# Turning queries and keys with block transfers and one VectorE transpose in a two-layer decoder trunk

## The chip, the cores and the metric

The kernel runs on one core of a Trainium2 chip. The time of a run is device microseconds (us). The engines of the core work side by side, each through its own list of instructions in order: TensorE (PE in the profile; PEld is its weight load), VectorE (DVE), ScalarE (ACT), GpSimd (POOL) and SyncE (SP), which issues the transfers.

## What is computed

A residual stream x of 256 rows and 2048 columns passes through two layers. Each layer norms x, projects it onto queries, keys (in the second layer forget gates), values and a gate for each of 32 heads, mixes within each head, and projects the result back. Cut to the lines that matter here:

```python
def even_layer(x, norm_g, w_in, q_gain, k_gain, w_out):
    proj = jnp.einsum('bsd,de->bse', rms_norm(x, norm_g), w_in)
    qa, ka, va, qb, kb, vb, gate = split_cols(proj, ...)
    oa = stick_breaking_attention(to_heads(qa), to_heads(ka), to_heads(va))   # 16 heads
    ob = dilated_attention(to_heads(qb), to_heads(kb), to_heads(vb), q_gain, k_gain)  # 16 heads
    mix = jnp.concatenate([oa, ob], axis=-1) * jax.nn.silu(gate)
    return x + jnp.einsum('bse,ed->bsd', mix, w_out)

def odd_layer(x, norm_g, w_in, lb, o_gain, w_out):
    proj = jnp.einsum('bsd,de->bse', rms_norm(x, norm_g), w_in)
    q, f_pre, inp, gate = split_cols(proj, ...)
    o = hgrn2(to_heads(q), to_heads(f_pre), to_heads(inp), lb)                # 32 heads
    mix = rms_norm(o, o_gain) * jax.nn.silu(gate)
    return x + jnp.einsum('bse,ed->bsd', mix, w_out)
```

Both attentions multiply queries with keys over the 128 head columns, and hgrn2 forms its scores from queries and keys with running products of the forget gates along the rows. Each of these wants the head's columns on the 128 partitions, while the projection leaves its rows there.

## The kernel before

For each head a product of 16 steps (`product`, L247) adds 128x512 matmuls into two PSUM tiles `acc`, one for each half of the 256 rows. The 512 columns are the head's query, key or forget gate, value and gate, 128 each. A step is six matmuls. The weights come in pairs of steps: one transfer (`raw`, L200), one ScalarE cast to the high part (`whi`, L211) and one VectorE subtraction to the low part (`wlo`, L212). Four buffers each of `raw`, `whi` and `wlo` are in use, so the cast for pair p+4 waits until TensorE is done with pair p. Here the pairs of a head are called pair 0 to pair 7.

The work that follows a head's product runs beside the product of the next head. It is a Python generator; `Side.tick` resumes it between steps, and `yield n` puts it off by n steps. A scheduler then fixes the order of each engine's list. Each head goes through these places:

- `evacuate` (L272) copies `acc`, scaled, to an SBUF tile `pj`, two ScalarE instructions of 512 columns.
- `flip_pair` (L140) transposes query and key with four TensorE transposes against `ident` into one PSUM tile (`flip`, L137); ScalarE then copies them to SBUF.
- A stick-breaking head (L305) multiplies them at L313 and L314, a dilated head (L338) at L358 and L359.
- An hgrn head (L390) takes sigmoids of the forget gate, then runs a chain of about 20 VectorE instructions from L401 to L454 that makes `sp`, `qk` and `qv`, and TensorE forms two sets of scores from them at L461 (the second one from `qv`).
- `weighted_values` (L295) and `emit_mix` (L291) end the head; the latter transposes the result `sg`.

Of the kernel before, what the change touches and what calls it, by code (L numbers as in the profile page):

```python
# [10 lines left out]
F32 = mybir.dt.float32  # L11
# [23 lines left out]
def hybrid_trunk(  # L35
# [16 lines left out]
    nc = tc.nc  # L52
    const = ctx.enter_context(tc.tile_pool(name="const", bufs=1))
# [15 lines left out]
    lbr = const.tile([P, 2, NH], F32, name="lbr")  # L69
    ones = const.tile([P, SEQ], F32, name="ones")  # L70
    nc.vector.memset(ones, 1.0)
    ident = const.tile([P, P], F32, name="ident")
# [67 lines left out]
    def flip_pair(pj):  # L140

        ps = flip([pj[:, t, c * P : (c + 1) * P] for c in range(2) for t in range(NT)])
        return ps.rearrange("p (c t) -> p c t", c=2)

# [133 lines left out]
    def gate_exp(pj):  # L278

        g = pj[:, :, 384:512]  # L280
# [13 lines left out]

    def weighted_values(at0, at1, at11, pj, c):  # L295


        o = psb.tile([P, NT, P], F32, name="att")
        v = pj[:, :, c * P : (c + 1) * P]
        nc.tensor.matmul(o[:, 0, :], at0, v[:, 0, :], start=True, stop=True)  # L300
        nc.tensor.matmul(o[:, 1, :], at1, v[:, 0, :], start=True, stop=False)  # L301
        nc.tensor.matmul(o[:, 1, :], at11, v[:, 1, :], start=False, stop=True)  # L302
        return o

    def stick_breaking(h, pj):  # L305
        sg = gate_exp(pj)
        yield 4
        ps = flip_pair(pj)
        qk = work.tile([P, 2, SEQ], F32, name="qk", bufs=2)
        nc.scalar.copy(qk, ps)  # L310
        yield 3
        zp = psb.tile([P, 384], F32, name="att")
        nc.tensor.matmul(zp[:, 0:128], qk[:, 0, 0:P], qk[:, 1, 0:P], start=True, stop=True)  # L313
        nc.tensor.matmul(zp[:, 128:384], qk[:, 0, P:], qk[:, 1, :], start=True, stop=True)  # L314
        z = work.tile([P, 384], F32, name="wt", bufs=2)
        nc.vector.scalar_tensor_tensor(
            z, zp, 1.0 / math.sqrt(P), strict, op0=ALU.mult, op1=ALU.add
        )
        sp = work.tile([P, 384], F32, name="qv", bufs=2)
        nc.scalar.activation(sp, z, AF.Abs)  # L320
        nc.scalar.activation(sp, sp, AF.Exp, scale=-1.0)
        nc.scalar.activation(sp, sp, AF.Ln, bias=1.0)
        nc.vector.scalar_tensor_tensor(sp, z, 0.0, sp, op0=ALU.max, op1=ALU.add)

        for lo, hi in ((0, 128), (128, 384)):
            back = sp[:, lo:hi][:, ::-1]
            nc.vector.tensor_tensor_scan(back, ones[:, 0 : hi - lo], back, 0.0, ALU.mult, ALU.add)
# [5 lines left out]
        o = weighted_values(at[:, 0:128], at[:, 128:256], at[:, 256:384], pj, 2)  # L333
        nc.vector.tensor_mul(sg, o, sg)
        yield 2
        emit_mix(h, sg, 1.0)

    def dilated(h, pj):  # L338
        sg = gate_exp(pj)
        qv = pj[:, :, 0:256].rearrange("p t (c d) -> p t c d", c=2)  # L340
        sq = work.tile([P, NT, 2, P], F32, name="sp", bufs=2)
# [6 lines left out]
        for t in range(NT):  # L348
            sl = pj[:, t, P : 2 * P]
# [7 lines left out]
        z = psb.tile([P, 384], F32, name="att")  # L357
        nc.tensor.matmul(z[:, 0:128], qk[:, 0, 0:P], qk[:, 1, 0:P], start=True, stop=True)  # L358
        nc.tensor.matmul(z[:, 128:384], qk[:, 0, P:], qk[:, 1, :], start=True, stop=True)  # L359
        nm = small.tile([P, NT], F32, name="nm")  # L360
# [20 lines left out]
        yield 3  # L381
        o = weighted_values(at[:, 0:128], at[:, 128:256], at[:, 256:384], pj, 2)
        for t in range(NT):
# [5 lines left out]

    def hgrn(h, pj):  # L390
        g = pj[:, :, 384:512]
# [12 lines left out]
        nc.scalar.activation(kk, fp, AF.Sigmoid, scale=-1.0)  # L404
        q = work.tile([P, SEQ], F32, name="qt", bufs=2)
        nc.scalar.copy(q, ps[:, 0, :])
        nc.scalar.activation(kk, kk, AF.Copy, scale=oml[:, h : h + 1])

        def blocks(a, n):
            return a.rearrange("p (b n) -> p b n", n=n)  # L410

# [30 lines left out]
        qq, cross = qc[:, 0:SEQ], qc[:, SEQ:]  # L442
        nc.vector.tensor_mul(qq, q, f)

# [75 lines left out]
        yield 2  # L520
        o = weighted_values(at[:, 0, :], cross, at[:, 1, :], pj, 2)
        so = small.tile([P, NT], F32, name="so")
# [178 lines left out]
```

## Time and profile before

| what | value |
|---|---|
| median of 3 runs | 1967.46 us (1967.27 to 1967.49) |
| profiled execution | 1967.47 us |
| its span | 1965.7 us |
| PE busy | 1956.2 us (100%) |
| DVE busy | 1286.5 us (65%) |
| ACT busy | 1038.3 us (53%) |
| POOL busy | 55.9 us (3%) |
| DMA moved | 344.39 MB, mean 175 GB/s |

The span reaches from the first instruction to the last. The profiled execution took 1.77 us more than its span. The granted clock was 1.0 (of 2.4 GHz) throughout.

### The profile page before, as it was taken

How to read it: one execution, taken by the hardware profiler on the slowest of the kernel's cores; microseconds unless marked ns; L12 is line 12 of the kernel's file. 1: busy time of each engine (PE TensorE's matmuls, PEld its weight loads, DVE VectorE, ACT ScalarE, POOL GpSimd, SP SyncE). 2: the span in 40 equal slices, each digit the busy share in tenths (PEclk: the TensorE clock that was granted, in tenths of full speed). 3: DMA queues.
4: the chain of work that ended last, by engine and by line, in shares of the span. 5: the costliest groups of instructions: out<-in, count | busy, mean ns of one | idle time of the engine just before them, and what ended most of it. 6: DMA issues, size and time to landing. Idle time of an engine off the chain costs nothing.

```text
span 1965.7 us, 25693 instructions
## 1 busy us (share of the span) xinstructions
PE 1956.2 (100%) x9280; PEld 1611.5 (82%) x9280; DVE 1286.5 (65%) x2456; ACT 1038.3 (53%) x1653; POOL 55.9 (3%) x54
## 2 busy tenths in 40 slices
PE   8999999999999999999999999999999999999999
PEld 7888888888888888888888888888888888888887
DVE  6666666666666666555577777777777777776444
ACT  6555555555555555444455555555555555555432
POOL 0000000000000000000000000000000000000000
PEclk9999999999999999999999999999999999999999
DMA  9555555555555555555554544555555544455664
GB/s 324 166 178 175 173 174 177 173 172 175 177 173 173 175 176 172 181 183 192 187 177 161 162 160 161 172 161 165 166 163 162 165 162 160 158 169 164 200 204 139
DMA packets 97407, 344.39 MB, mean 175 GB/s; under 512 B 11136, under 2 KB 12288, under 8 KB 97280
## 3 DMA queue, kind: packets, MB, share of 16 engines
q1 hardware_dynamic: 97136, 342.73, 54.0%
q8 instruction: 73, 1.20, 0.2%
q14 instruction: 54, 0.44, 0.1%
q10 hardware_dynamic: 144, 0.02, 0.0%
HBM read 340.61 MB, written 2.10 MB: 174 GB/s over the span
## 4 chain that ended last, share of the span: by engine, by line
PE 100%; DMA 0%; ACT 0%; DVE 0%; DVEq 0%; issue 0%
PE acc L254 30%; PE acc L256 30%; PE acc L255 30%; PE att L137 3%; PE att L461 2%; PE att L490 1%; PE att L301 1%; PE att L302 1%; PE att L300 1%; PE att L518 0%; PE att L359 0%; PE att L314 0%; DMA gn<-in_gains 0%; PE att L313 0%; PE att L358 0%; ACT xh L128 0%
## 5 line engine op out<-in xcount | busy, mean ns | idle before, releaser
L212 DVE TENSOR_TENSOR wlo<-raw,whi 128x1024 fp32r<-128x1024 f32 (+1 forms) x642 | 782.2, 1219 | 545.2 <-ACT whi L211 543.8
L211 ACT CAST whi<-raw 128x1024 fp32r<-128x1024 f32 (+1 forms) x642 | 673.2, 1049 | 631.6 <-PE acc L256 547.2
L254 PE MATMUL acc<-whi,xh 128*128 128x512 f32 x2048 | 837.4, 409 | 5.8 <-ACT whi L211 5.8
L256 PE MATMUL acc<-whi,xl 128*128 128x512 f32 x2048 | 802.6, 392 | 0.0
L255 PE MATMUL acc<-wlo,xh 128*128 128x512 f32 x2048 | 800.1, 391 | 0.0
L256 PEld LDWEIGHTS acc<-whi,xl 128*128 128x128 f32 x2048 | 384.9, 188 | 84.9
L254 PEld LDWEIGHTS acc<-whi,xh 128*128 128x128 f32 x2048 | 385.7, 188 | 79.0 <-ACT whi L211 5.8
L255 PEld LDWEIGHTS acc<-wlo,xh 128*128 128x128 f32 x2048 | 386.3, 189 | 72.0 <-DVE wlo L212 0.6
L254 PE MATMUL acc<-whi,mixh 128*128 128x512 f32 x512 | 201.8, 394 | 0.0
L256 PE MATMUL acc<-whi,mixl 128*128 128x512 f32 x512 | 199.5, 390 | 0.0
L255 PE MATMUL acc<-wlo,mixh 128*128 128x512 f32 x512 | 199.3, 389 | 0.0
L256 PEld LDWEIGHTS acc<-whi,mixl 128*128 128x128 f32 x512 | 96.1, 188 | 20.3
L255 PEld LDWEIGHTS acc<-wlo,mixh 128*128 128x128 f32 x512 | 96.2, 188 | 19.4
L254 PEld LDWEIGHTS acc<-whi,mixh 128*128 128x128 f32 x512 | 96.2, 188 | 19.3
L275 ACT ACTIVATE pj<-acc,rstd 128x512 f32<-128x512 f32 x128 | 87.5, 685 | 30.6 <-PE acc L256 30.1
L285 DVE RECIPROCAL sg<-sg 128x256 f32<-128x256 f32 x32 | 56.0, 1749 | 0.5
L179 POOL TENSOR_TENSOR rr<-rv,mhalf 128x4 f32<-128x4 f32 x16 | 29.3, 1833 | 716.0 <-DVE rv L178 716.0
L179 POOL TENSOR_TENSOR ro<-rv,mhalf 128x2 f32<-128x2 f32 x32 | 25.0, 780 | 831.0 <-DVE pr L474 808.0
L504 ACT COPY ri<-qk 128x128 f32<-128x128 f32 x32 | 9.6, 299 | 58.4 <-DVE qk L413 58.4
L137 PE MATMUL att<-ident,pj 128*128 128x128 f32 x256 | 38.5, 272 | 0.0
L413 DVE TENSOR_TENSOR qk<-qk 128x128 f32<-128x128 f32 x128 | 37.0, 289 | 2.2
L429 DVE RECIPROCAL ri<-qk 128x160 f32<-128x160 f32 x32 | 36.7, 1148 | 0.0
(141 smaller groups left out, 1272.3 us busy)
## 6 DMA issues: line engine op xcount, KB each, us to landing
raw<-in_w_odd SPq DMA_DIRECT2D x256, 512.0 KB, 3.6
raw<-in_w_even SPq DMA_DIRECT2D x254, 512.0 KB, 3.5
raw<-in_w_out SPq DMA_DIRECT2D x128, 512.0 KB, 3.5
xres<-in_xt SPq DMA_DIRECT2D x8, 256.0 KB, 7.3
xres<-in_x SPq DMA_DIRECT2D x4, 512.0 KB, 7.3
out<-xres SPq DMA_DIRECT2D x6, 256.0 KB, 5.1
raw<-in_w_even SPq DMA_DIRECT2D x4, 256.0 KB, 4.8
out<-xres SPq DMA_DIRECT2D x4, 128.0 KB, 2.0
```

What stands on the lines that cost most here:

```text
L137: nc.tensor.transpose(ps[:, i * P : (i + 1) * P], b, ident)
L179: nc.gpsimd.tensor_tensor(dst, v[:, 0:n], mhalf[:, 0:n], op=ALU.pow)
L211: nc.scalar.copy(hi[:, s, :], half[:, s, :])
L212: nc.vector.tensor_sub(lo[:, s, :], half[:, s, :], hi[:, s, :].bitcast(F32))
L254: nc.tensor.matmul(acc[t], sh[:, k, s], hi, start=(k == 0), stop=False)
L255: nc.tensor.matmul(acc[t], sh[:, k, s], lo, start=False, stop=False)
L256: nc.tensor.matmul(acc[t], sl[:, k, s], hi, start=False, stop=(k == nk - 1))
L275: nc.scalar.activation(pj[:, t, :], acc[t], AF.Copy, scale=rstd[:, t : t + 1])
L285: nc.vector.reciprocal(sg, sg)
L413: nc.vector.tensor_tensor(o, a, b.broadcast_to(list(o.shape)), op=ALU.mult)
L429: nc.vector.reciprocal(ri, f8[:, :, 3:8])
L461: nc.tensor.matmul(ps[:, t, :], kt[:, t * P : (t + 1) * P], qt[t], start=True, stop=True)
```

## The change

Queries and keys leave PSUM into a tile of their own (`qkp`), values and gates into another (`pj`, half as wide). 16 SBUF-to-SBUF transfers for each head, issued from SP, each move one 32-row by 32-column block of four 128x128 squares to its transposed place in a tile `mvp` (one buffer). One VectorE transpose then turns each 32x32 block. The last head of the dilated group and the last hgrn head keep the TensorE transposes (`quick`). The yields around the place change: in a stick-breaking head 4 before the flips becomes 2 before the moves and 4 before the turn, in a dilated head 8 becomes 5 and 4, in an hgrn head 3 becomes 2 and 4. A vector of 256 ones becomes one element that is broadcast.

```diff
+    def move_blocks(src, name):
+        n = src.shape[2] // P
+        moved = work.tile([P, NT, n, 4, 32], F32, name=name, bufs=1)
+        to = moved.rearrange("p t c a j -> p (t c) a j")
+        v = src.rearrange("p t (c f) -> p (t c) f", f=P)
+        for a in range(4):
+            for b in range(4):
+                nc.sync.dma_start(
+                    to[32 * b : 32 * b + 32, :, a, :], v[32 * a : 32 * a + 32, :, 32 * b : 32 * b + 32]
+                )
+        return moved
+    def turn_blocks(dst, moved):
+        nc.vector.transpose(dst, moved.rearrange("p t c a j -> p (t c a j)"))
+    def turn_pair(qk, quick):
+        if quick:
+            ps = flip([qk[:, t, c * P : (c + 1) * P] for t in range(NT) for c in range(2)])
+            nc.scalar.copy(qk, ps.rearrange("p (t f) -> p t f", t=NT))
+        else:
+            moved = move_blocks(qk, "mvp")
+            yield 4
+            turn_blocks(qk.rearrange("p t f -> p (t f)"), moved)
...
     def evacuate(acc, rstd):
-        pj = work.tile([P, NT, 512], F32, name="pj", bufs=2)
-        for t in range(NT):
-            nc.scalar.activation(pj[:, t, :], acc[t], AF.Copy, scale=rstd[:, t : t + 1])
-        return pj
+        qk = work.tile([P, NT, 256], F32, name="qkp", bufs=2)
+        vg = work.tile([P, NT, 256], F32, name="pj", bufs=2)
+        for dst, c in ((qk, 0), (vg, 256)):
+            for t in range(NT):
+                nc.scalar.activation(
+                    dst[:, t, :], acc[t][:, c : c + 256], AF.Copy, scale=rstd[:, t : t + 1]
+                )
+        return qk, vg
...
-    def stick_breaking(h, pj):
-        sg = gate_exp(pj)
-        yield 4
-        ps = flip_pair(pj)
-        qk = work.tile([P, 2, SEQ], F32, name="qk", bufs=2)
-        nc.scalar.copy(qk, ps)
+    def stick_breaking(h, qk, vg):
+        sg = gate_exp(vg)
+        yield 2
+        yield from turn_pair(qk, False)
         yield 3
...
-        yield 8
-        ps = flip_pair(pj)
-        qk = work.tile([P, 2, SEQ], F32, name="qk", bufs=2)
-        nc.scalar.copy(qk[:, 0, :], ps[:, 0, :])
-        nc.scalar.activation(qk[:, 1, :], ps[:, 1, :], AF.Copy, scale=qkg)
+        yield 5
+        yield from turn_pair(qk, h == NH - 1)
+        k = qk[:, :, P:]
+        nc.scalar.activation(k, k, AF.Copy, scale=qkg)
         yield 3
...
-        yield 3
-        ps = flip_pair(pj)
-        fp = ps[:, 1, :]
+        yield 2
+        yield from turn_pair(qk, h == NH - 1)
+        q, fp = qk[:, :, 0:P], qk[:, :, P:]
         fk = work.tile([P, 2, SEQ], F32, name="qk", bufs=2)
         f, kk = fk[:, 0, :], fk[:, 1, :]
-        nc.scalar.activation(f, fp, AF.Sigmoid)
+        nc.scalar.activation(blocks(f, P), fp, AF.Sigmoid)
```

The order of the lists changes with it. On SP, in an hgrn head of the second layer, only weight loads stood before. Now the 16 moves stand between loads like this (L148 is a move, L223 a weight load):

```order
L148 DMA mvp<-qkp 32x4x32 x2
L223 DMA raw<-in_w_odd 128x1024
L148 DMA mvp<-qkp 32x4x32 x3
L223 DMA raw<-in_w_odd 128x1024
L148 DMA mvp<-qkp 32x4x32 x11
L223 DMA raw<-in_w_odd 128x1024 x6
```

The second load, for pair 0 of the head after, waits until VectorE has subtracted pair 4. The 11 moves behind it wait with it. A stick-breaking head has 2, 5 and 9 moves around its two loads, a dilated head 3 and 13 around one.

On DVE, the chain of an hgrn head began like this before, with the subtraction of pair 5 (L212) ahead of it:

```order
L212 TENSOR_TENSOR wlo<-raw,whi 128x1024
L401 TENSOR_SCALAR qk<-qk,oml,lbc 128x256
L421 TENSOR_TENSOR qk<-qk 128x128
L422 TENSOR_TENSOR qk<-qk 128x128
L413 TENSOR_TENSOR qk<-qk 128x64x2 x2
```

Now the transpose stands behind the subtraction of pair 7 (the second of the `x2`), and the chain behind that of pair 0 of the next product. Between its first instructions stand the head before's norm (`rv`, then `ro` on GpSimd) and its two products with `ro`:

```order
L235 TENSOR_TENSOR wlo<-raw,whi 128x1024 x2
L155 STREAM_TRANSPOSE qkp<-mvp 128x512
L235 TENSOR_TENSOR wlo<-raw,whi 128x1024
L432 TENSOR_SCALAR qk<-qk,oml,lbc 128x256
L201 TENSOR_SCALAR rv<-so 128x2
L558 SCALAR_TENSOR_TENSOR sg<-att,ro,sg 128x128
L447 TENSOR_TENSOR qk<-qk 128x128
L558 SCALAR_TENSOR_TENSOR sg<-att,ro,sg 128x128
L448 TENSOR_TENSOR qk<-qk 128x128
```

The chain's start has moved by three pairs against the product that runs beside it. Its end, on DVE, stands like this now; the last row makes the part of `qv` that the second scores need:

```order
L439 TENSOR_TENSOR qk<-qk 128x32x4
L235 TENSOR_TENSOR wlo<-raw,whi 128x1024
L469 TENSOR_TENSOR wt<-qkp,qk 128x256
L235 TENSOR_TENSOR wlo<-raw,whi 128x1024
L439 TENSOR_TENSOR qv<-wt,tots 128x8x16
L129 SCALAR_TENSOR_TENSOR mixl<-att,hg,mixh 128x256
L439 TENSOR_TENSOR qv<-qv,tots 128x8x8
```

The product with `mixl` (the head before's result, which TensorE turns at the end of pair 7) now stands between the two rows of `qv`; before, it came after both. On PE the scores keep their distance from the head before's weighted values: 42 matmuls of the product and the two transposes of `sg` between them, before and now.

## Rows read from the trace of the kernel before

**Rows 1.** The chain of work that ended last, on the page: shares of the span.
```profile
PE 100%; DMA 0%; ACT 0%; DVE 0%; DVEq 0%; issue 0%
```
**Rows 2.** Groups by line: busy us, mean ns of one | idle us before, what ended it.
```profile
L212 DVE TENSOR_TENSOR wlo<-raw,whi 128x1024 fp32r<-128x1024 f32 (+1 forms) x642 | 782.2, 1219 | 545.2 <-ACT whi L211 543.8
L211 ACT CAST whi<-raw 128x1024 fp32r<-128x1024 f32 (+1 forms) x642 | 673.2, 1049 | 631.6 <-PE acc L256 547.2
```
**Rows 3.** Timeline of PE in a stick-breaking head: start us, us, engine, line.
```profile
301.31 0.49 PE L137 MATMUL att<-ident,wt 128*128 128x128 f32 x3
...
303.03 0.60 PE L137 MATMUL att<-ident,pj 128*128 128x128 f32 x4
303.39 0.48 PE L254 MATMUL acc<-whi,xh 128*128 128x512 f32 x1
303.70 0.40 PE L255 MATMUL acc<-wlo,xh 128*128 128x512 f32 x1
```
**Rows 4.** Timeline of DVE in the same head, around pair 4.
```profile
301.07 1.16 DVE L212 TENSOR_TENSOR wlo<-raw,whi 128x1024 fp32r<-128x1024 f32 x1
```
**Rows 5.** Timeline of PE, layer 1: values of one head, scores of the next.
```profile
1405.63 0.38 PE L300 MATMUL att<-pj,at 128*128 128x128 f32 x2
...
1406.22 0.47 PE L254 MATMUL acc<-whi,xh 128*128 128x512 f32 x1
...
1414.51 0.38 PE L137 MATMUL att<-ident,sg 128*128 128x128 f32 x2
...
1416.12 0.60 PE L461 MATMUL att<-sp 128*128 128x128 f32 x4
1416.56 0.82 PE L461 MATMUL att<-qv,qk 128*128 128x192 f32 x4
```
**Rows 6.** Timeline of ACT in the same stretch.
```profile
1401.02 1.05 ACT L211 CAST whi<-raw 128x1024 fp32r<-128x1024 f32 x1 [1.32 <-PE acc L256]
1401.97 0.38 ACT L400 ACTIVATE qk<-att 128x256 f32<-128x256 f32 x1
...
1406.90 0.28 ACT L525 ACTIVATE junk<-att 128x128 bf16<-128x128 f32 x1
1407.07 0.19 ACT L525 ACTIVATION_READ_ACCUMULATOR junk<-att 128x1 f32 x1
...
1416.32 1.04 ACT L211 CAST whi<-raw 128x1024 fp32r<-128x1024 f32 x1 [0.91 <-PE acc L256]
```
**Rows 7.** Timeline of DVE in the same stretch.
```profile
1404.11 0.29 DVE L422 TENSOR_TENSOR qk<-qk 128x128 f32<-128x128 f32 x1
...
1407.44 1.22 DVE L212 TENSOR_TENSOR wlo<-raw,whi 128x1024 fp32r<-128x1024 f32 x1
1408.58 0.42 DVE L443 TENSOR_TENSOR wt<-qt,qk 128x256 f32<-128x256 f32 x1
1408.91 0.17 DVE L178 TENSOR_SCALAR rv<-so 128x2 f32<-128x2 f32 x1
...
1417.39 1.23 DVE L212 TENSOR_TENSOR wlo<-raw,whi 128x1024 fp32r<-128x1024 f32 x1 [0.18 <-ACT whi L211]
```
**Rows 8.** Timeline of POOL in the same stretch.
```profile
1409.22 0.70 POOL L179 TENSOR_TENSOR ro<-rv,mhalf 128x2 f32<-128x2 f32 x1 [25.11 <-DVE pr L474]
```
**Rows 9.** Groups by line: the full-width VectorE work nearest to the transpose.
```profile
L342 DVE TENSOR_TENSOR sp<-pj 128x512 f32<-128x512 f32 x16 | 11.0, 685 | 0.0
L285 DVE RECIPROCAL sg<-sg 128x256 f32<-128x256 f32 x32 | 56.0, 1749 | 0.5
```
**Rows 10.** Timeline of SP: small transfers issued one behind the other.
```profile
16.00 0.42 SPq L87 DMA_DIRECT2D ident<-in_eye  x1
16.48 0.42 SPq L88 DMA_DIRECT2D strict<-in_cmask  x1
```
**Rows 11.** Transfers by line: KB each, median us from issue to landing.
```profile
out<-xres SPq DMA_DIRECT2D x4, 128.0 KB, 2.0
```
**Rows 12.** DMA queues on the page: packets, MB, share of 16 engines.
```profile
q1 hardware_dynamic: 97136, 342.73, 54.0%
```

More of the change, by code (lines that the diff above doesn't have):

```diff
@@ L69, in hybrid_trunk @@
     lbr = const.tile([P, 2, NH], F32, name="lbr")
-    ones = const.tile([P, SEQ], F32, name="ones")
-    nc.vector.memset(ones, 1.0)
+    one = const.tile([P, 1], F32, name="one")
+    nc.vector.memset(one, 1.0)
     ident = const.tile([P, P], F32, name="ident")
@@ L138, in flip @@
         return ps
-    def flip_pair(pj):
-        ps = flip([pj[:, t, c * P : (c + 1) * P] for c in range(2) for t in range(NT)])
-        return ps.rearrange("p (c t) -> p c t", c=2)
+    def move_blocks(src, name):
[19 more added lines that the diff above has]
+            turn_blocks(qk.rearrange("p t f -> p (t f)"), moved)
     def flip_weights(w):
@@ L293, in emit_mix, with weighted_values @@
         split_into(mixh[:, h, :], mixl[:, h, :], flip([mix[:, t, :] for t in range(NT)]), scale)
-    def weighted_values(at0, at1, at11, pj, c):
+    def weighted_values(at0, at1, at11, vg):
         o = psb.tile([P, NT, P], F32, name="att")
-        v = pj[:, :, c * P : (c + 1) * P]
+        v = vg[:, :, 0:P]
         nc.tensor.matmul(o[:, 0, :], at0, v[:, 0, :], start=True, stop=True)
@@ L303, in weighted_values, with products @@
         return o
-    def stick_breaking(h, pj):
-        sg = gate_exp(pj)
-        yield 4
-        ps = flip_pair(pj)
-        qk = work.tile([P, 2, SEQ], F32, name="qk", bufs=2)
-        nc.scalar.copy(qk, ps)
+    def products(qk):
+        ps = psb.tile([P, 384], F32, name="att")
+        k = qk[:, :, P:]
+        nc.tensor.matmul(ps[:, 0:128], qk[:, 0, 0:P], k[:, 0, :], start=True, stop=True)
+        nc.tensor.matmul(ps[:, 128:384], qk[:, 1, 0:P], k, start=True, stop=True)
+        return ps
+    def stick_breaking(h, qk, vg):
+        sg = gate_exp(vg)
+        yield 2
+        yield from turn_pair(qk, False)
         yield 3
-        zp = psb.tile([P, 384], F32, name="att")
-        nc.tensor.matmul(zp[:, 0:128], qk[:, 0, 0:P], qk[:, 1, 0:P], start=True, stop=True)
-        nc.tensor.matmul(zp[:, 128:384], qk[:, 0, P:], qk[:, 1, :], start=True, stop=True)
+        zp = products(qk)
         z = work.tile([P, 384], F32, name="wt", bufs=2)
@@ L326, in stick_breaking @@
             back = sp[:, lo:hi][:, ::-1]
-            nc.vector.tensor_tensor_scan(back, ones[:, 0 : hi - lo], back, 0.0, ALU.mult, ALU.add)
+            nc.vector.tensor_tensor_scan(back, one.broadcast_to([P, hi - lo]), back, 0.0, ALU.mult, ALU.add)
         nc.vector.tensor_sub(z, z, sp)
@@ L336, in stick_breaking, with dilated @@
         emit_mix(h, sg, 1.0)
-    def dilated(h, pj):
-        sg = gate_exp(pj)
-        qv = pj[:, :, 0:256].rearrange("p t (c d) -> p t c d", c=2)
+    def dilated(h, qk, vg):
+        sg = gate_exp(vg)
+        qv = qk.rearrange("p t (c d) -> p t c d", c=2)
         sq = work.tile([P, NT, 2, P], F32, name="sp", bufs=2)
@@ L348, in dilated @@
         for t in range(NT):
-            sl = pj[:, t, P : 2 * P]
+            sl = qk[:, t, P:]
             nc.vector.tensor_scalar_mul(sl, sl, rr[:, 2 * t + 1 : 2 * t + 2])
-        yield 8
-        ps = flip_pair(pj)
-        qk = work.tile([P, 2, SEQ], F32, name="qk", bufs=2)
-        nc.scalar.copy(qk[:, 0, :], ps[:, 0, :])
-        nc.scalar.activation(qk[:, 1, :], ps[:, 1, :], AF.Copy, scale=qkg)
+        yield 5
+        yield from turn_pair(qk, h == NH - 1)
+        k = qk[:, :, P:]
+        nc.scalar.activation(k, k, AF.Copy, scale=qkg)
         yield 3
-        z = psb.tile([P, 384], F32, name="att")
-        nc.tensor.matmul(z[:, 0:128], qk[:, 0, 0:P], qk[:, 1, 0:P], start=True, stop=True)
-        nc.tensor.matmul(z[:, 128:384], qk[:, 0, P:], qk[:, 1, :], start=True, stop=True)
+        z = products(qk)
         nm = small.tile([P, NT], F32, name="nm")
@@ L388, in dilated, with blocks, hgrn @@
         emit_mix(h, sg, 1.0)
-    def hgrn(h, pj):
-        g = pj[:, :, 384:512]
+    def blocks(a, n):
+        return a.rearrange("p (b n) -> p b n", n=n)
+    def hgrn(h, qk, vg):
+        g = vg[:, :, P:]
         sg = work.tile([P, NT, P], F32, name="sg")
@@ L403, in hgrn @@
         )
-        nc.scalar.activation(kk, fp, AF.Sigmoid, scale=-1.0)
-        q = work.tile([P, SEQ], F32, name="qt", bufs=2)
-        nc.scalar.copy(q, ps[:, 0, :])
+        nc.scalar.activation(blocks(kk, P), fp, AF.Sigmoid, scale=-1.0)
         nc.scalar.activation(kk, kk, AF.Copy, scale=oml[:, h : h + 1])
-        def blocks(a, n):
-            return a.rearrange("p (b n) -> p b n", n=n)
         def times(o, a, b):
@@ L442, in hgrn @@
         qq, cross = qc[:, 0:SEQ], qc[:, SEQ:]
-        nc.vector.tensor_mul(qq, q, f)
+        nc.vector.tensor_mul(blocks(qq, P), q, blocks(f, P))
         qv = work.tile([P, 8, 48], F32, name="qv", bufs=2)
@@ L520, in hgrn @@
         yield 2
-        o = weighted_values(at[:, 0, :], cross, at[:, 1, :], pj, 2)
+        o = weighted_values(at[:, 0, :], cross, at[:, 1, :], vg)
         so = small.tile([P, NT], F32, name="so")
@@ L550, in head @@
     def head(layer, h, acc):
-        pj = evacuate(acc, rstds[layer])
+        qk, vg = evacuate(acc, rstds[layer])
         if layer == 1:
-            yield from hgrn(h, pj)
+            yield from hgrn(h, qk, vg)
         elif h < NSB:
-            yield from stick_breaking(h, pj)
+            yield from stick_breaking(h, qk, vg)
         else:
-            yield from dilated(h, pj)
+            yield from dilated(h, qk, vg)
     def residual(layer, n, acc, ssq):
```

10 lines of the change are left out of this document (5 added, 5 removed).

## The prediction

> **What bounds the kernel now.** I read the chain of work that ended last first: it runs on TensorE for the whole span [rows 1], so a microsecond taken from TensorE's list is a microsecond gained, unless TensorE then has to wait. The groups by line say who waits: ScalarE's casts of the weights stood idle 547.2 us for TensorE to release a buffer, and VectorE's subtractions 543.8 us for those casts [rows 2]. Both engines run ahead of TensorE by up to four pairs and have slack on average. The change must therefore be read in two ways: what it takes from TensorE, and whether any result that TensorE needs now comes too late at its place in the list.
>
> **What it takes away.** 62 of the 64 heads lose four transposes (16 stick-breaking, 15 dilated, 31 hgrn). From the start of the four transposes to the start of the second matmul behind them is 0.67 us (303.03 to 303.70) [rows 3]. A plain matmul takes 0.23: 36 of them lie between 1406.22 and 1414.51 [rows 5]. So four transposes cost 0.67 - 0.23 = 0.44 us of TensorE, and 62 x 0.44 = 27.3 us go. The Trainium skill, VectorE: DVE Perf Modes, "Rules for kernel authors", speaks against the change: it keeps a 128x128 transpose on TensorE where PSUM will do as its destination, and "The three transpose paths" gives 390 ns for one in bf16. Priced by that, 248 transposes would be an estimated 97 us and the gain alone would lead to 1871 us; the trace, 110 ns of the path for each, does not bear it out.
>
> **Edits I cost at nothing.** ScalarE evacuates in four instructions in place of two but no longer copies queries and keys out of PSUM; VectorE gets 62 block transposes. The nearest row to the transpose is the full-width product, 0.69 us for 512 columns, and the far one a reciprocal, 1.75 us for 256, so 3.5 for 512 [rows 9]. I take 0.69, since a transpose computes nothing. 62 x 0.69 = 43 us lie in VectorE's 545 us of idle time [rows 2]; without that cover they would cost the 43. The transfers add 62 x 16 x 128 = 126,976 packets of 128 bytes, 16.3 MB. By bytes that is 4.7% of what the queue moves, or 3% more of the engines' time; at the mean cost of a packet now (54.0% for 97,136) it would be 71% more, over the limit [rows 12]. Those packets carry 3.5 KB each, so I take the end near the bytes.
>
> **Where a wait could come in: the moves.** They are issued one by one on SP. The nearest rows are 0.48 us apart, with one run per row [rows 10]; a move has four runs on each side, so 0.48 is the low end, and I take 0.6. A 128 KB transfer lands 2.0 us after its issue [rows 11]; I take that for 16 KB. In a stick-breaking head the load ahead of the last nine moves waits for pair 4's subtraction, done at 301.07 + 1.16 = 302.23 [rows 4]. With 0.48 for the load and 0.6 for the moves, the last starts at 307.5 and lands at 309.5. VectorE gets there behind pair 7's subtraction, and TensorE wants the result in its pair 5. Pair 1 ends at 301.31 [rows 3]. Pair 2 and the three transposes of `wt` (3 x 0.11) bring 304.4, pair 3 307.2. Then come 0.20 to the cast and 1.07 from cast to subtraction [rows 5 to 7], 1.14 until the next VectorE instruction [rows 7], about 0.35 for the product with `sg`: the transpose starts at 309.9 and ends at 310.6. TensorE arrives after half a pair, 0.59 of values [rows 5], half a pair and three matmuls, at 311.2. So nothing waits here; 0.4 us are left before the moves are late for VectorE, and 0.6 before the transpose is late for TensorE. By the issue time of a move, stick-breaking heads start to wait at about 0.71 us. The same count gives 0.66 in dilated heads, where all 16 moves wait for the scaled keys, and 0.67 in hgrn heads with eleven behind the held load. The loads behind the moves leave some 5 us later than now, still ahead of their casts.
>
> **Where a wait does come in: the hgrn chain.** Here the place in the list, not the transfer, decides. TensorE needs the second scores' `qv` 10.93 us after it begins the head before's values (1405.63 to 1416.56) [rows 5], and that distance stays. The chain now stands behind the subtraction of pair 0 of the next product, whose buffer comes free exactly where those values begin. From there: 0.20 to the cast, 1.07 to the subtraction, 1.14 to the next instruction, so VectorE's chain opens at 2.41. ScalarE, after the cast (0.95) [rows 6], takes two sigmoids and a scaling of at most 0.38 each and two squares of 0.28 + 0.19, so `rv` can come at 3.23. GpSimd starts 0.31 after `rv` and takes 0.70 [rows 7, 8]; VectorE, next in line for `ro`, stands until 4.25. Three instructions of 0.29 bring the chain's third row (L448) to 5.1; from there to the subtraction ahead of `wt` took 3.33 (1404.11 to 1407.44), that subtraction 1.14, `wt` 0.33, another subtraction 1.14 [rows 7]: 11.05. `qv`, `mixl` and `qv` again at 0.29, 0.42 and 0.29 end at 12.05. That is 1.1 us too late. It is the upper bound, because it adds whole durations where rows show the next instruction starting early: 0.95 after a cast of 1.05, 0.17 after a square of 0.28 [rows 6], 1.14 after a subtraction of 1.22 [rows 7]. Some eleven such overlaps, small ones of 0.04 mostly, take off about 0.45. I take a wait of 0.65 us for each of the 31 hgrn heads: 20.2 us. The lower bound is no wait, if about 1.1 us of this list overlaps. The same wait shifts the next head as a whole, so it does not grow.
>
> **The sum.** 27.3 taken away, 20.2 given back: 1967.47 - 7.1 = 1960.4 us, against the profiled execution's own time (its span is 1965.7), which is the median to 0.01. Layer 0 keeps its 13.6 us; layer 1 gains 13.6 and loses 20.2.
>
> **Rivals.** *All of it stays hidden:* the hgrn chain overlaps enough. For it speaks that the ScalarE and VectorE idle shares are large; against it that the chain is serial and its order fixed. It gives 1967.5 - 27.3 = 1940.
>
> *The moves land late (the other side).* If SP needs 0.75 us for a move, the waits are 8 x 0.04 in 16 heads, 15 x 0.09 in 15 and 10 x 0.08 in 31: 5 + 20 + 25 = 50 us, so 2010. It decides from about 0.68 us, where 9 us eat the rest of the gain; each 0.1 us beyond costs some 66 us. For it speaks that no row shows a transfer of this shape; against it that the row is 0.48. The Trainium skill, DMA: Bandwidth & Descriptors, "Rules for kernel authors", warns that transfers under 64 KB are mostly overhead; "Anatomy of one DMA" puts the fixed part at about 2.0 us. Sixteen that did not overlap would by that be an estimated 32 us a head. The rows agree with the 2.0, yet they show issues 0.48 us apart, so no such string is to be expected.
>
> *VectorE's transpose is slow.* At 3.5 us it would be late by 2.3 us in layer 0's 31 heads and about 2 in layer 1's: 130 us, near 2090. *The transfer engines fill up:* by the mean packet cost, the program would run at 125% of them, above 2400 us. Both need the far end of their bounds.
>
> **How the numbers follow.** The forecast's own case (a wait of 0.3 to 1.0 in hgrn heads, 1950 to 1972) gets 0.36, all hidden 0.25, late moves 0.30, a slow transpose 0.05, full engines 0.04. 0.2% is 3.9 us here, about what a measurement can tell from no change, so faster means under 1963.5 and slower above 1971.4. Faster: 0.25 and 0.22 of the forecast's case, 0.47. Within: 0.11 of it and 0.04 of late moves that just balance, 0.15. Slower: 0.38. The range goes from all hidden (1938) to late moves at 0.75 us (2012); what is left out is the worse half of the late moves and the two far cases. The forecast's own range is 1950 to 1972.
>
> **What would show it.** In the profile of the changed kernel: no wait of TensorE on layer 0's products; in layer 1 a wait of 0.3 to 1.0 us at the second scores for VectorE's `qv`; GpSimd's `ro` ahead of a stand of VectorE of about 1 us; moves some 0.6 us apart on SP; the block transpose near 0.7 us; the transfer share only a few points above 54%. The prediction is wrong if moves stand over 0.68 us apart, if VectorE waits for transfers at the transpose, if the transpose takes over 1.3 us, or if TensorE waits at a place I have not named.

## The result, and the profile after

The changed kernel takes 1994.01 us (median of 4 runs, 1992.49 to 1995.66) against 1967.37 for the kernel before on the same chip: ratio 1.0136, 95% interval 1.0118 to 1.0153. It is slower by 26.6 us, where 7.1 us faster was forecast. The profiled execution's span is 1993.9 us, 28.2 more than before.

The page after: busy times, the transfers' queue (packets, MB, share of 16 engines), the chain that ended last:

```profile
PE 1945.4 (98%) x9032; PEld 1587.2 (80%) x9032; DVE 1319.1 (66%) x2518; ACT 1010.2 (51%) x1719; POOL 53.3 (3%) x54
...
q1 hardware_dynamic: 239984, 359.05, 57.9%
...
PE 55%; DVE 18%; SPq 10%; issue 7%; ACT 5%; DMA 4%; POOL 1%; DVEq 0%; ACTq 0%; POOLq 0%
```

Before, the chain was TensorE alone [rows 1]. Now it leaves TensorE for 45% of the span: it runs through SP's issues, VectorE and transfers. Which places those are, TensorE's own waits say (waits of PE: us in total, times, longest):

```profile
PE att L336 <- ACT qkp L385: 18.2, 15, 2.0
PE att L487 <- DVE pr L500: 12.4, 31, 1.0
PE acc L277 <- ACT whi L234: 6.1, 1, 6.1
PE att L336 <- DVE qkp L155: 5.2, 6, 2.2
```

L336 is the product of queries and keys: it waits in all 15 dilated heads, for ScalarE's scaling of the turned keys, and in six stick-breaking heads for the block transpose itself. L487 is the second scores of the 31 hgrn heads. The third row is at the program's beginning and belongs to kernels with and without moves.

The costs of the new work, from the groups by line (busy us, mean ns, idle before):

```profile
L155 DVE STREAM_TRANSPOSE qkp<-mvp 128x512 f32<-128x512 f32 x62 | 44.1, 711 | 49.7 <-DMA mvp<-qkp 49.6
```

from the instructions of line 148 (minimum, median and maximum in ns):

```profile
L148 SPq DMA_DIRECT2D mvp<-qkp x992: 585/599/1706, 44.0 to 1795.2; - x199
```

and from the transfers (KB, median us from issue to landing):

```profile
mvp<-qkp SPq DMA_DIRECT2D x992, 16.0 KB, 2.1
```

The transpose is 0.71 us, a move is 0.60 in the median on SP and lands in 2.1, and the transfer engines went from 54.0 [rows 12] to 57.9%: singly, each was forecast well. But VectorE stands 49.6 us at the transposes for moves.

Where the time went is read from the start of each head's evacuation. These are the rows of ScalarE's timeline, after, for heads 4, 16, 31, 33 and 62 (numbered through both layers; 16 is the first dilated, 33 the second hgrn head):

```profile
131.09 0.46 ACT L300 ACTIVATE qkp<-acc,rstd 128x256 f32<-128x256 f32 x1
...
422.62 0.46 ACT L300 ACTIVATE qkp<-acc,rstd 128x256 f32<-128x256 f32 x1
...
801.57 0.48 ACT L300 ACTIVATE qkp<-acc,rstd 128x256 f32<-128x256 f32 x1
...
1026.77 0.47 ACT L300 ACTIVATE qkp<-acc,rstd 128x256 f32<-128x256 f32 x1 [0.98 <-PE acc L279]
...
1780.65 0.47 ACT L300 ACTIVATE qkp<-acc,rstd 128x256 f32<-128x256 f32 x1
```

and the same five in the kernel before:

```profile
125.66 0.69 ACT L275 ACTIVATE pj<-acc,rstd 128x512 f32<-128x512 f32 x1 [0.99 <-PE acc L256]
...
416.62 0.69 ACT L275 ACTIVATE pj<-acc,rstd 128x512 f32<-128x512 f32 x1 [0.99 <-PE acc L256]
...
779.82 0.69 ACT L275 ACTIVATE pj<-acc,rstd 128x512 f32<-128x512 f32 x1 [0.91 <-PE acc L256]
...
1006.61 0.69 ACT L275 ACTIVATE pj<-acc,rstd 128x512 f32<-128x512 f32 x1
...
1754.99 0.69 ACT L275 ACTIVATE pj<-acc,rstd 128x512 f32<-128x512 f32 x1
```

Their differences give an account by stage (the last two columns are experiments told below):

| stretch | before | after | after less before | no moves | 12 moves, later gate and products |
|---|---|---|---|---|---|
| to head 4 | 125.66 | 131.09 | +5.4 | 123.84 | 124.92 |
| 12 stick-breaking heads, each | 24.25 | 24.29 | +0.6 in all | 23.76 | 23.76 |
| 15 dilated heads, each | 24.21 | 25.26 | +15.8 in all | 23.78 | 23.89 |
| heads 31 to 33 | 226.8 | 225.2 | -1.6 | 225.2 | 223.5 |
| 29 hgrn heads, each | 25.81 | 26.00 | +5.5 in all | 25.34 | 25.34 |
| rest | 210.7 | 213.3 | +2.5 | 211.6 | 211.6 |

Layer 0 is the surprise: 21.8 us lost by the end of the dilated heads, where 13.6 were to be gained. Layer 1 loses 6.4 us, about the 6.6 (20.2 less 13.6) of the forecast.

**A stick-breaking head after.** SP, VectorE and TensorE in head 15, one of the eight of the twelve that run without trouble (timelines):

```profile
400.68 1.24 SPq L148 DMA_DIRECT2D mvp<-qkp  x2
402.01 0.54 SPq L223 DMA_DIRECT2D raw<-in_w_even  x1
402.61 3.17 SPq L148 DMA_DIRECT2D mvp<-qkp  x5
405.87 0.53 SPq L223 DMA_DIRECT2D raw<-in_w_even  x1
406.45 5.74 SPq L148 DMA_DIRECT2D mvp<-qkp  x9
```
```profile
404.22 1.16 DVE L235 TENSOR_TENSOR wlo<-raw,whi 128x1024 fp32r<-128x1024 f32 x1
...
413.65 0.71 DVE L155 STREAM_TRANSPOSE qkp<-mvp 128x512 f32<-128x512 f32 x1 [0.62 <-DMA mvp<-qkp]
```
```profile
414.02 0.40 PE L279 MATMUL acc<-whi,xl 128*128 128x512 f32 x1
414.51 0.46 PE L336 MATMUL att<-qkp 128*128 128x128 f32 x2
```

From 400.68 to 412.19 SP has no break: 16 moves and two loads stand 0.58 to 0.69 us apart. The load ahead of the last nine moves could go at 405.38, when pair 4's subtraction (the row at 404.22) is done, but SP comes to it only at 405.87. The last move starts near 411.6 and lands 2.05 later, at the transpose's start. Matmuls follow each other 0.23 apart, so L336 was due at 414.25 and comes 0.26 late. The list of waits doesn't show this one, since matmul ends in the trace are modelled and a short gap hides in them: read starts. In heads 9 to 12 one of SP's issues takes some 0.5 to 0.7 us longer than usual (a load takes 1.18 and 1.24 in heads 9 and 10, the nine moves 6.41 and 6.20 in heads 11 and 12), and the products there come 0.7 to 0.95 late.

**A dilated head after.** SP, VectorE, ScalarE, TensorE:

```profile
584.36 1.89 SPq L148 DMA_DIRECT2D mvp<-qkp  x3
586.34 0.53 SPq L223 DMA_DIRECT2D raw<-in_w_even  x1
586.92 8.32 SPq L148 DMA_DIRECT2D mvp<-qkp  x13
```
```profile
584.05 0.28 DVE L381 TENSOR_SCALAR qkp<-qkp,rr 128x128 f32<-128x128 f32 x1
...
596.58 0.71 DVE L155 STREAM_TRANSPOSE qkp<-mvp 128x512 f32<-128x512 f32 x1 [0.90 <-DMA mvp<-qkp]
```
```profile
574.48 1.05 ACT L234 CAST whi<-raw 128x1024 fp32r<-128x1024 f32 x1 [1.63 <-DMA raw<-in_w_even]
575.43 0.47 ACT L300 ACTIVATE qkp<-acc,rstd 128x256 f32<-128x256 f32 x1
...
577.10 0.98 ACT L399 ACTIVATE sp<-sp,nm,rr 128x128 f32<-128x128 f32 x2
577.99 0.46 ACT L300 ACTIVATE qkp<-acc,rstd 128x256 f32<-128x256 f32 x1
...
597.33 0.51 ACT L385 ACTIVATE qkp<-qkp,qkg 128x256 f32<-128x256 f32 x1 [2.91 <-DVE qkp L155]
```
```profile
597.89 0.49 PE L336 MATMUL att<-qkp 128*128 128x128 f32 x2 [0.94 <-ACT qkp L385]
```

All 16 moves start behind the scaled keys, here 0.64 us apart, and everything from the keys (L381) to the products is one string of 13.8 us. The keys themselves are no later than before against the evacuation: they are done 8.90 us behind its start, before the change 8.82, although the softmax (L399, 0.98) of the head before now stands on ScalarE ahead of the evacuation's second half. But the evacuation starts late. ScalarE's cast ahead of it (the row at 574.48) waits 1.63 us for a weight load that stood on SP behind the 13 moves of the head before; it waits so, 1.28 to 1.63 us, in every head from 17 to 30. Against the last matmul of its product the evacuation starts 0.1 to 0.4 us later than before the change.

### The profile page after: what moved, and what is told of

Read it like the earlier page. It is cut to its first block, busy times and chain, and to the rows that moved or that the text cites. A ratio compares the mean times of both kernels' runs of the same rounds, so it can differ in the third digit from the quotient of the medians.

```text
span 1993.9 us, 26825 instructions
## 1 busy us (share of the span) xinstructions
PE 1945.4 (98%) x9032; PEld 1587.2 (80%) x9032; DVE 1319.1 (66%) x2518; ACT 1010.2 (51%) x1719; POOL 53.3 (3%) x54
## 3 DMA queue, kind: packets, MB, share of 16 engines
q1 hardware_dynamic: 239984, 359.05, 57.9%
## 4 chain that ended last, share of the span: by engine, by line
PE 55%; DVE 18%; SPq 10%; issue 7%; ACT 5%; DMA 4%; POOL 1%; DVEq 0%; ACTq 0%; POOLq 0%
PE acc L277 17%; PE acc L279 17%; PE acc L278 17%; SPq L148 10%; DVE wlo L235 5%; ACT whi L234 4%; DMA raw<-in_w_even 2%; DVE qk L439 2%; DVE ri L455 2%; PE att L487 1%; DMA mvp<-qkp 1%; PE att L516 1%; POOL ro L202 1%; DVE sg L312 1%; DVE wt L469 1%
## 5 line engine op out<-in xcount | busy, mean ns | idle before, releaser
L155 DVE STREAM_TRANSPOSE qkp<-mvp 128x512 f32<-128x512 f32 x62 | 44.1, 711 | 49.7 <-DMA mvp<-qkp 49.6
L300 ACT ACTIVATE qkp<-acc,rstd 128x256 f32<-128x256 f32 x128 | 60.4, 474 | 12.3 <-PE acc L279 9.3
L300 ACT ACTIVATE pj<-acc,rstd 128x256 f32<-128x256 f32 x128 | 60.2, 472 | 0.0
L439 DVE TENSOR_TENSOR qk<-qk,tots 128x128 f32<-128x128 f32 x64 | 18.5, 288 | 43.0 <-PE att L516 42.9
L558 DVE SCALAR_TENSOR_TENSOR sg<-att,ro,sg 128x128 f32<-128x128 f32 x64 | 22.1, 349 | 27.8 <-POOL ro L202 27.8
```

The source lines that it names most:

```text
L155: nc.vector.transpose(dst, moved.rearrange("p t c a j -> p (t c a j)"))
L300: nc.scalar.activation(dst[:, t, :], acc[t][:, c : c + 256], AF.Copy, scale=rstd[:, t : t + 1])
L439: nc.vector.tensor_tensor(o, a, b.broadcast_to(list(o.shape)), op=ALU.mult)
```

## The experiments

Where nothing else is said, a kernel differs from the changed one by the lines shown. Times are medians of 4 or more runs; each had the kernel before on its chip, at 1967.2 to 1967.4. The us of a dilated head are means over heads 17 to 30, behind the first of the stage.

**Without moves.**
```
- moved = move_blocks(qk, "mvp")
  yield 4
- turn_blocks(qk.rearrange("p t f -> p (t f)"), moved)
+ turn_blocks(qk.rearrange("p t f -> p (t f)"), still)   # a constant tile
```


> The 16 moves of a head are left out: the block transpose stays at its place and reads a constant tile, so queries and keys are not the reference's. Everything else, the split evacuation, the block transposes and the yields, is as in the changed kernel. Theory A (the transfers are the cause: moves reach the block transpose late, and loads queued behind them on SP reach their casts late): layer 0 then shows the full saving, 31 x 0.44 = 13.6 us, the stall at heads 2 to 3 is gone, and hgrn heads keep +0.15 us each (-0.44 and +0.59 at the second scores), since there the order on VectorE makes the wait: 1967.4 - 13.6 + 4.6 = 1958. Rival B (the hgrn wait comes from the moves as well): 1967.4 - 27.3 = 1940. Rival C (the transfers are not the cause; the extra evacuations, the block transposes and the moved places in the program are): it stays near 1994.


Measured: 1938.54 us, ratio 0.9855 (0.984 to 0.9869). It is the full saving, 28.8 us, 0.46 for each of 62 heads: four transposes cost 0.115 us each, where [rows 3] gave 0.11. The split evacuation and 62 transposes on VectorE cost TensorE nothing, so C falls. The number is B's, but B does not follow: without moves to wait for, the block transpose was listed earlier in VectorE's order too, in hgrn heads at 11.9 us ahead of the head before's values where it was 0.3 ahead. The kernel thus changes two things there, and the hgrn wait needed its own test.

**The hgrn wait.**
```
-     nc.gpsimd.tensor_tensor(dst, v[:, 0:n], mhalf[:, 0:n], op=ALU.pow)
+     nc.vector.reciprocal(dst, v[:, 0:n])               # for ro alone
```


> As the changed kernel, but in hgrn heads the norm's factor is a reciprocal on VectorE in place of the power on GpSimd (the square root is left out, so the output is not the reference's). VectorE's order is otherwise the same, row for row, and no transfer changes. Theory (the hgrn wait of 0.59 us at the second scores is VectorE's chain, which stands 0.87 us for GpSimd's factor): that stand goes, the wait with it, 31 x 0.59 = 18 us: 1976. Rival B (the hgrn wait comes from moves that land late): within 3 us of 1994.


Measured: 1977.05 us, ratio 1.0048 (1.0033 to 1.0063): 17 us less than the changed kernel. Hgrn heads take 25.35 in place of 25.96, and the second scores follow the first without a gap (timeline of TensorE; in the changed kernel the second row came 0.98 behind the first):

```profile
1356.39 0.60 PE L490 MATMUL att<-sp 128*128 128x128 f32 x4
1356.83 0.82 PE L490 MATMUL att<-qv,qk 128*128 128x192 f32 x4
```

No transfer was touched. The theory stands: the wait is VectorE's chain with its stand for GpSimd. The changed kernel's own trace agrees: in heads 58 to 62 the transpose does not wait for its moves at all, and the heads take 25.95 us as elsewhere.

**Products and scores asked for one step later.**
```
  yield from turn_pair(qk, False)
- yield 3
+ yield 4        # the same in dilated heads; 10 to 11 ahead of the first scores
```


> As the changed kernel, but TensorE asks one step (six matmuls, 1.4 us) later: at the products of queries and keys in layer 0 and at the first and second scores in layer 1. Nothing is left out. Theory A1 (what costs is that the moved and turned tile comes some tenths of a microsecond after TensorE asks): the waits of 0.3 to 0.9 us at the products and of 0.59 us at the scores go; 27.3 us saved less the stall of 6.3 us at heads 2 to 3 and 2.4 us at the end, so 1948, and with a few waits left at most 1955. Theory A2 (what costs in layer 0 is that loads behind the moves leave SP late, so casts wait): layer 0 keeps its +20, layer 1 gains 31 x 0.44 = 13.6, so about 1976. Rival (the later place only pushes the rest of the chain against the next head): 1990 or more.


Measured: 1977.18 us, ratio 1.0054 (1.0039 to 1.0069). The number is A2's (about 1976), but the stages are not A2's: in the profiled run layer 0 keeps 18 of its 21.8 us, but layer 1 gains 6 and not 13.6. Stick-breaking heads without trouble fall to 23.83, and many hgrn heads to 25.35, as A1 says. Dilated heads stay at 25.23: there the products kept their place in TensorE's list (the same row of the list, since the scheduler already put them later than the program asks). In the middle of layer 1 hgrn heads take up to 26.6: SP issues 13 moves in a row there, in 8.3 us as a rule and in 10.4 ahead of the first slow head. Why those issues took longer is not told apart.

**Every second move on ScalarE.**
```
- nc.sync.dma_start(
+ (nc.sync, nc.scalar)[b % 2].dma_start(
```


> As the changed kernel, but every second move of a head is issued by ScalarE in place of SP. Nothing is left out. Theory A (SP's issue of 0.71 us a move makes moves and loads late): eight moves a queue take 5.7 us in place of 11.4, so layer 0's waits and the stall at heads 2 to 3 go, and hgrn keeps +0.15 a head: about 1958. Rival D (the landing or the transfer engines limit the moves, not the issue): no change, 1994. Rival E (ScalarE holds the casts; eight issues of 0.6 to 0.7 us, some 5 us a head, push casts back): slower than the changed kernel, 2000 to 2060.


Measured: 2002.89 us (1995.39 to 2009.5), ratio 1.0193 (1.0175 to 1.021). Both A and E are right, in different stages. Stick-breaking heads lose all their wait (23.76). Dilated heads go to some 26, since ScalarE now issues moves in place of casts (timeline of ACT in a dilated head):

```profile
577.84 6.95 ACTq L148 DMA_DIRECT2D mvp<-qkp  x8
584.82 2.95 ACT L234 CAST whi<-raw 128x1024 fp32r<-128x1024 f32 x3 [7.62 <-PE att L137]
```

**All moves on GpSimd.**
```
- nc.sync.dma_start(
+ nc.gpsimd.dma_start(
```


> As the changed kernel, but all 16 moves of a head are issued by GpSimd, whose queue is otherwise empty; SP's queue holds only loads again, as before the change. Nothing is left out. Theory A2 (loads late behind moves): the stall at heads 2 to 3 goes, and casts no longer wait for loads. If GpSimd's issue costs no more than SP's 0.71 us, moves come about as late as now, so SB and dilated heads keep part of their wait: 1967 to 1985. If GpSimd takes 1 us or more for a move, moves take 16 us or more a head and TensorE waits for each: 16 x 0.3 = 5 us a head beyond now, above 2150.


Measured: 2041.04 us, ratio 1.0373 (1.0352 to 1.0395): between the two cases. GpSimd's issue is cheap, 0.55 us, so the first case's condition holds, but its 1967 to 1985 does not. A move lands 3.5 us after its issue in the median. In dilated heads (28.4 us each) the moves wait for the scaled keys as on SP, and then stand still between groups (timeline of POOL):

```profile
538.80 1.87 POOL L202 TENSOR_TENSOR rr<-rv,mhalf 128x4 f32<-128x4 f32 x1 [15.56 <-DVE rv L201]
541.77 2.76 POOL L148 DMA_DIRECT2D mvp<-qkp  x5 [1.10 <-DVE qkp L381]
546.70 4.34 POOL L148 DMA_DIRECT2D mvp<-qkp  x8 [2.17 <-issue]
```

What the stand of 2.17 us is, the trace does not tell.

**A quarter of the bytes.**
```
- to[32*b : 32*b+32, :, a, :],   v[32*a : 32*a+32, :, 32*b : 32*b+32]
+ to[32*b : 32*b+32, 0:1, a, :], v[32*a : 32*a+32, 0:1, 32*b : 32*b+32]
```


> As the changed kernel, but each of the 16 moves carries one of its four runs a row: 4 KB in place of 16, 32 packets in place of 128; three quarters of queries and keys are a constant. Theory A (the price is SP's time for each issue, 0.6 us whatever it carries): moves stay some 0.64 us apart and the time stays near 1994. Rival (the issue's price follows the packets that it describes, or bytes limit): moves come 0.2 to 0.4 us apart and the waits of layer 0 go: 1945 to 1965.


Measured: 1965.97 us, ratio 0.9993 (0.9984 to 1.0002). By the issue A is right: 0.59 in the median for 4 KB against 0.60 for 16, landing 2.4 against 2.1. SP's price is for the instruction, not for what it carries (4 or 16 KB). By the time the rival is right: stick-breaking heads take 23.77, dilated 24.02. But the time does not speak for the rival's cause. The quarter that is moved is the queries of the first 128 rows, so these moves wait neither for the second half of the evacuation nor for the scaled keys. In a dilated head they start 0.50 us behind the evacuation (which is at 558.79 here), where the keys are done 8.8 behind it (timelines of SP and VectorE):

```profile
559.29 0.51 SPq L150 DMA_DIRECT2D part<-qkp  x1
...
569.16 4.30 SPq L150 DMA_DIRECT2D part<-qkp  x7
```
```profile
567.13 0.48 DVE L383 TENSOR_SCALAR qkp<-qkp,rr 128x128 f32<-128x128 f32 x2 [0.57 <-POOL rr L204]
```

Seven moves in a row still stand 0.63 us apart. So layer 0 can be free here because the moves start early; bytes and start were changed together, and the run does not separate them. Hgrn heads stay at 25.96, which fits the test above; the stall at the start stays too (head 4 at 129.86).

**Twelve moves.**
```
+ if a == b:
+     nc.gpsimd.tensor_copy(dst, blk)
+ else:
      nc.sync.dma_start(dst, blk)
```


> As the changed kernel, but the four blocks on the diagonal, which stay on their partitions, are copied by GpSimd; SP issues 12 moves a head in place of 16. Nothing is left out. Theory A (SP's issues make moves and loads late): 4 x 0.64 = 2.6 us less a head on SP, more than the 0.3 us (SB) and some 1 us (dilated) by which the products wait, so layer 0 gets its 13.6 us; the stall at heads 2 to 3 falls from 6 to about 3. VectorE's order in hgrn heads changes with it (the block transpose's chain stands ahead of the norm), so that wait may go too: 1945, or 1963 if it stays. Rival (not the number of issues but landing or bytes, or the engines' order in layer 0): 1985 to 1994.


Measured: 1955.03 us, ratio 0.9936 (0.992 to 0.9953), faster than the kernel before. Stick-breaking 23.76 and hgrn 25.35, both free; dilated still 24.74, for which the 1945 of the theory is missed by 10. The number of issues on SP is what held stick-breaking heads: TensorE asks for their products three matmuls earlier than in the changed kernel and still does not wait.

**Dilated heads on TensorE.**
```
- yield from turn_pair(qk, h == NH - 1)
+ yield from turn_pair(qk, True)            # dilated only
```


> As the changed kernel, but the dilated heads turn queries and keys by TensorE transposes and one copy by ScalarE; stick-breaking and hgrn heads as changed. Nothing is left out. Theory A (dilated heads lose most, since all their moves wait for the scaled keys): they go back from 25.25 us a head to the 24.21 of before, 15 x 1.04 = 16 us: 1978. Rival (the loss belongs to the stage's place in the program or to the split evacuation): dilated heads stay above 24.8 and the time above 1986.


Measured: 1980.93 us, ratio 1.0068 (1.0053 to 1.0083): dilated heads 24.21, as before the change. The loss belongs to their moves.

**The first three heads on TensorE.**
```
- yield from turn_pair(qk, False)
+ yield from turn_pair(qk, h < 3)
```


> As the changed kernel, but heads 0 to 2 turn queries and keys on TensorE. Nothing is left out. Theory (in the first heads the loads behind the moves have no lead yet, so the casts of head 3 wait 6.6 us for them): the 30.5 us between heads 2 and 3 fall to 24.2, 6.3 us less, and 1 us more for transposes: 1988.5. Rival (the stall belongs to the first heads that issue moves, wherever they stand): within 2 us of 1994.


Measured: 1990.1 us (1986.72 to 1992.6), ratio 1.0115 (1.01 to 1.013). Head 4 comes at 126.5 in place of 131.1. The stall of the changed kernel, in rows of SP and ACT:

```profile
88.72 8.96 SPq L148 DMA_DIRECT2D mvp<-qkp  x14
97.79 1.95 SPq L223 DMA_DIRECT2D raw<-in_w_even  x4
```
```profile
101.98 1.05 ACT L234 CAST whi<-raw 128x1024 fp32r<-128x1024 f32 x1 [6.58 <-DMA raw<-in_w_even]
```

The loads behind head 2's 14 moves leave SP 9 us later for them, and while the buffers are not yet ahead, a cast waits.

**The gate of dilated heads behind the keys**, in the changed kernel and with twelve moves:
```
- sg = gate_exp(vg)          # first in dilated()
  ...
- yield 5
+ yield 2
+ sg = gate_exp(vg)
+ yield 3
```


> As the changed kernel, but in dilated heads the gate (its product, exponential and reciprocal, some 2.4 us of VectorE) is placed behind the scaling of the keys, for which all 16 moves wait, in place of ahead of it. Nothing is left out and no transfer changes. Theory A' (dilated heads run at 25.25 us because one chain goes round: scaled keys, 16 moves, block transpose, scaling, products, softmax, and VectorE reaches the next head's keys only behind that softmax and the gate; longer than TensorE's 23.8): 2.4 us off that loop bring it under TensorE's work, 15 x 1.45 = 22 us: 1972, and no wait at the products. Rival (TensorE waits because SP's moves are too slow for this stage wherever they start): 1988 to 1994.


Measured: 1992.95 us, ratio 1.0132 (1.0117 to 1.0147). A' fails as written: the keys were ready 7.15 us after the evacuation's start in place of 8.9, but the products moved forward in TensorE's list by 8 matmuls, and TensorE still waited there, 16.4 us in 15 heads after 18.2.

> Twelve moves a head with the diagonal blocks copied by GpSimd, and the gate of dilated heads behind the scaled keys. Nothing is left out. If the waits are understood, what is left over the 1938.5 of the kernel without moves is the start: stick-breaking 23.76, dilated 23.8 in place of 24.73, hgrn 25.35: 1955.0 - 15 x 0.93 = 1941. If SP's time for the moves holds dilated heads back by itself, 1950 to 1955.


Measured: 1944.43 us, ratio 0.9884 (0.9869 to 0.9899); dilated heads 24.04 where 23.8 was expected, about the 3.4 us over 1941.

**The products of dilated heads later**, by 8 matmuls in the changed kernel; by 10 with the later gate; by 5 with twelve moves and the later gate:
```
  nc.scalar.activation(k, k, AF.Copy, scale=qkg)
- yield 3
+ yield 6        # 5 with the later gate, 4 with twelve moves as well
```


> As the changed kernel, but the products of dilated heads stand 8 matmuls (1.8 us) later in TensorE's list; the gate stays ahead of the scaled keys. Nothing is left out. Theory P (TensorE just asks 0.94 us too early): the wait goes, 15 x 1.45 = 22 us: 1972. Rival L (the loop: later products put this head's softmax and with it the next head's keys, moves and products later by as much): the wait stays, 1988 to 1996.


Measured: 1985.4 us, ratio 1.0089 (1.0072 to 1.0106); dilated heads 24.68. Some 0.6 of the 1.5 us a head goes, so neither P nor L holds alone. What takes back the rest reads as a loop, though not L's: it runs through the loads behind the moves (timeline of ACT):

```profile
645.07 1.05 ACT L234 CAST whi<-raw 128x1024 fp32r<-128x1024 f32 x1 [1.50 <-DMA raw<-in_w_even]
646.03 0.46 ACT L300 ACTIVATE qkp<-acc,rstd 128x256 f32<-128x256 f32 x1
```

The cast ahead of the next evacuation waits again for its load. Against the last matmul of its product the evacuation starts 2.3 to 4.2 us later than before the change in heads 17 to 30, where it was 0.1 to 0.4 in the changed kernel. The next keys, moves and products come later with it. No run tests this loop by itself. From keys to transpose it is now 12.8 to 13.9 us (12.3 in the head above), since two loads stand among the moves in place of one.

> As the changed kernel with the gate of dilated heads behind the scaled keys, and their products asked for two steps later, which puts them 10 matmuls (2.3 us) further down TensorE's list. Nothing is left out. Theory P (with the gate moved, the products' place in the list moved 8 matmuls forward too and took the gain back; TensorE just asks 0.84 us too early): the wait goes and dilated heads take 23.8: 1993 - 15 x 1.25 = 1974. Rival (moves on SP hold the stage whatever the place): 1988 or more.


Measured: 1982.12 us, ratio 1.0075 (1.006 to 1.009); dilated heads 24.59. Again a part: the same cast waits for the same load, and the evacuation starts 0.4 to 0.8 us later than before the change in most heads.

> As the kernel with twelve moves and the later gate, and the products of dilated heads asked for one step later (5 matmuls, 1.15 us). Nothing is left out. Theory P: the last wait of 0.22 us in dilated heads goes, 15 x 0.22 = 3.3 us: 1941. Rival L: no change, 1944.


Measured: 1940.58 us, ratio 0.9864 (0.9849 to 0.9879). After the first heads of the stage dilated heads run at 23.78, and TensorE's waits are gone (waits of PE, all rows):

```profile
PE acc L280 <- ACT whi L237: 5.7, 1, 5.7
PE att L339 <- DVE qkp L158: 0.7, 1, 0.7
```

**The start, in the fast kernel**, heads 0 to 2 on TensorE with twelve moves and the later gate.


> As the kernel with twelve moves and the later gate, and heads 0 to 2 turn queries and keys on TensorE, so that no moves stand ahead of loads while the first buffers fill. Nothing is left out. Theory: the rest of the start's stall, some 3 us, goes, against 3 x 0.46 = 1.4 us of transposes: 1939.5. Rival (the stall only moves to the first head with moves): 1941 to 1943.


Measured: 1944.15 us, ratio 0.9881 (0.9865 to 0.9898), 0.3 less than the 1944.43 of twelve moves and the later gate. Neither number. Head 4 comes at 125.24 in place of 125.38, without moves at 123.84: of the stall 1.5 us was left, about what the transposes of three heads cost (1.4), and no stall shows at the first head with moves, as the rival has it.

## Why the prediction was wrong, by its own steps

**The saving** (27.3 us) was right: 28.8 with all waits gone.

**The hgrn wait** (20.2 us, 0.65 a head) was right in place, cause and size: hgrn heads gain 0.46 and lose 0.61, and with the stand for `ro` out of VectorE's chain the 0.61 is back.

**The edits costed at nothing** were right: evacuation, block transpose (0.71 for 0.69), landing, share of the engines.

**The step that failed is the price of the moves on SP**, "I take 0.6", with the slack counted from it: "So nothing waits here", and "Layer 0 keeps its 13.6 us". The waits are those of the rival of late moves, but not at its price. An issue takes 0.60, and from one move to the next it is 0.64. By the prediction's own limits (0.71 in stick-breaking heads, 0.66 in dilated ones) 0.64 should have cost nothing. So the limits were counted wrong as well: the price enters at more places than the prediction put it.

In a stick-breaking head the prediction priced the nine moves behind the load that waits for pair 4's subtraction, and let that load go as soon as the subtraction was done. In head 15 the last of the nine starts 6.22 us after the subtraction, where 5.28 were counted. Of these 0.94 us, 0.49 is the load's start: seven moves and a load ahead of it hold SP until 405.8, where 0.6 and 0.48 apiece would have had it free in time. 0.10 is the load's own issue (0.58 for 0.48), and 0.35 is the nine at 0.64. The transpose ends 0.61 later than counted. The slack was 0.6, TensorE comes 0.1 earlier than counted and starts 0.15 after the transpose: 0.26 late. With fewer issues on SP, twelve in all or eight, this wait was gone. The Trainium skill, DMA: Bandwidth & Descriptors, "Rules for kernel authors", which the prediction set aside for lack of such a string, calls transfers under 64 KB mostly overhead; the runs agree, 0.59 us of issue for 4 KB and 0.60 for 16.

**The slack of dilated heads** (late from 0.66) was counted too wide besides: at 0.64 a move the products of the head above are 1.1 us late (0.94 of it shows as idle time). The prediction gives only the 0.66, not its working. Counted from the start of the last matmul of a product, the keys are done at 8.57 in the kernel before, and TensorE asks at 21.52 in the changed one (the head above). With the prediction's durations (0.48, 2.0, 0.69) between them the limit comes out at 0.65 without ScalarE's scaling of the turned keys (L385, 0.51) and at 0.62 with it. So that step seems to have been left out; this is inferred. The other part is the evacuation that starts up to 0.4 us late behind its cast. Undoing the moves there gave all of the loss back (24.21), fewer moves or later products each a part, and both with the later gate all. So the stage was held by the number of issues, by the loads behind them and by where TensorE asks; how much each has of the 1.5 us a head is not separated.

**"Still ahead of their casts"** failed in layer 0: casts wait for loads of `in_w_even` 42.4 us in 24 places (waits of ACT).

```profile
ACT whi L234 <- DMA raw<-in_w_even: 42.4, 24, 6.6
```

In the first heads it is a stall that was in no term: head 3 follows head 2 after 30.5 us, without moves after 23.8, so it is 6.8 us; with three heads on TensorE head 4 came 4.6 us earlier. In dilated heads it makes the evacuation late.

The remaining 2.5 us behind the last hgrn heads were not followed up; 0.9 of them is there without moves too.

## What to carry to other kernels

Work taken off the bounding engine is a gain only where what replaces it arrives before that engine asks; sixteen small transfers on one queue are a string of 10 us at 4 KB as at 16, so count instructions first, with all that stands ahead of them on the queue, and copy in place what need not move. When a result arrives a little late everywhere, look at the place at which it is asked for: a scheduler that fixes the lists beforehand moves that place with each edit and can take back what the edit gave. Queue work that holds up loads is dear where the loads have no lead yet, and where a late load holds up more than its own cast, since an engine works in order.

## What the runs showed of the hardware that was not expected

A small transfer between partitions costs SP 0.60 us at 16 KB and 0.59 at 4 KB, where the whole-row loads from memory stood 0.48 apart [rows 10]; on ScalarE it costs 0.61, on GpSimd 0.55 with a landing of 3.5 us in place of 2.1. The 16 KB transfers stand 0.64 apart on SP. Single issues took up to 1.7 us in the changed kernel; what they stood for the runs do not tell.
